# Hybrid attention and recurrence block: where weight loads, a shift row and the first attention stand in the order

## The chip, the core and the metric

The kernel runs on one core of a Trainium2 chip. The time is that of one execution on the device in microseconds (us), as the median of several runs. TensorE (PE) does the matrix products, VectorE (DVE) and ScalarE (ACT) the elementwise work, GpSimd (POOL) some small operations and loads, and SyncE (SP) issues most of the DMA transfers. Each engine, and SP's queue too, takes its instructions in the order in which they were built; an instruction that waits holds up all that stand behind it on the same engine.

## The reference

The block computes one layer on 512 tokens of width 2048, in float32:

```
mod = silu(c) @ w_ada + b_ada                      # six rows of 2048: shift, scale, gate, twice
h   = rms_norm(x, norm1_w) * (1 + scale1) + shift1
aq, ak, av, gq, gf, gi, gg = split(h @ w_in)       # 7 x 1024 columns
attn = rms_norm(dilated_attention(rope(rms(aq)), rope(rms(ak)), av))
hg   = rms_norm(hgrn2(gq, gf, gi)) * silu(gg)      # gated linear recurrence, 8 heads
x    = x + gate1 * (concat(attn, hg) @ w_out)
h2   = rms_norm(x, norm2_w) * (1 + scale2) + shift2
x    = x + gate2 * (square(relu(h2 @ w_ff1)) @ w_ff2)
```

## The kernel before, in words

**Products.** Every float32 operand is split into a high part (a cast on ACT) and a low part (a subtraction on DVE), and each product is the sum of three matmuls: high by high, high by low, low by high. `load_w` (L186) loads two slices of 128 rows by 512 columns of a weight in one DMA of 512 KB into one of four buffers (`wraw`), and `_split` makes `whi` (L39, ACT) and `wlo` (L40, DVE) from each, in four buffers each. `project` (L368) runs over the 16 slices, the steps k: 12 matmuls a step into four PSUM banks, and ACT copies the banks out at the end. There are thirteen such passes over `w_in` after the first two column groups.

**Modulation rows.** The six rows `mod` are matrix by vector products on DVE. `gemv` (L116) loads 256 KB slices (`araw`) and adds each one, times one value per partition, to two accumulators (`acc`, L127 and L129). `to_cols` (L138) adds the two (L143) and has PE turn the row into columns with four transposes (L149); ACT sums them up (L152). Two of these rows, made by `shift_through` (L748), are not of `mod` but of shift1 times columns of `w_in`: the first groups of columns are multiplied before shift1 is known, and what shift1 adds to them is put in afterwards. One is for the forget gates f (columns from 4096), the next for the queries gq of the recurrence (from 3072), and a third (from 4608) stands first in the list `later`.

**Order.** All of this is written as Python generators. `project` calls `tick()` once a step, which advances the front of `tasks` (the recurrence of four heads, or the attention of four heads) by one piece, and `bg_step()` at a rate of 1.85 or 2 a step, which advances `bgw` (the modulation rows). From the first pass after the column groups on (`hv0`, columns from 5120) PE's order is the order in which the code was traced (`manual_schedule`). On the other engines and on SP a scheduler sets the order when the program is built, from priorities and from its own model of time; `load_w` raises the priority of the weight loads. `issue_after(i)` keeps what is traced in its block behind instruction `i` on the same engine.

**Around the change.** The pass `hv0` runs with the shift rows from 4096 and 3072 in `bgw`. After it the recurrence `hgrn` of the first four heads is put into `tasks`; three passes later the attention of the first four heads, which runs through `hgrn_q(1)` (L558) and the next pass; then the second recurrence. In `attention` (L444), `scores` puts the products on DVE (L474, L476), then the exponentials on ACT (L478), `weights_t` transposes them on PE (L490) four pieces later, and `values` multiplies with v (L501).

Of the kernel before, what the change touches and what calls it, by code (L numbers as in the profile page):

```python
# [18 lines left out]
NK = D // P  # L19
# [25 lines left out]
def hybrid_block(ctx, tc, x, c, positions, norm1_w, w_ada, b_ada, w_in, q_norm_w, k_norm_w,  # L45
                 attn_out_norm_w, hg_lb_logits, hg_norm_w, w_out, norm2_w, w_ff1, w_ff2,
                 lnc, hgmask, inv_freq, out):
    nc = tc.nc
# [5 lines left out]
    win_v = w_in[0].rearrange("(k p) n -> p k n", p=P)  # L54
# [13 lines left out]
    def bank(name, tag="bg"):  # L68
        return ps.tile([P, 512], F32, name=name, tag=tag)
# [43 lines left out]
    pool.dma_start(ifq, inv_freq.broadcast_to([P, 16]))  # L113


    def gemv(view, vec, col0, n=512, early=False):  # L116

        accs = [(work("acc") if early else gv.tile([P, 512], F32, name="acc"))[:, 0:n] for _ in range(2)]
        nk = 512 // n
        for k0 in range(0, NK, nk):  # L120
            raw = spare.pop(0) if early and spare else slot("araw") if early else gv.tile([P, 512], F32, name="araw", bufs=4)
            raw = raw.rearrange("p (k n) -> p k n", n=n)
            nc.sync.dma_start(raw, view[:, k0:k0 + nk, col0:col0 + n])
            for k in range(k0, k0 + nk):
                acc = accs[k % 2]
                if k < 2:
                    dve.tensor_scalar(acc, raw[:, k - k0], vec[:, k:k + 1], None, op0=ALU.mult)  # L127
                else:
                    dve.scalar_tensor_tensor(acc, raw[:, k - k0], vec[:, k:k + 1], acc, op0=ALU.mult, op1=ALU.add)  # L129
            yield  # L130
        gemv.acc = accs
# [51 lines left out]
        nc.sync.dma_start(dst.rearrange("o (r p) -> (o r) p", p=P), row[0:NK, 0:P])  # L183
        yield

    def load_w(view, k0, c0, n=512, eng=None, ahead=True, raws=None):  # L186
        with tc.high_priority() if ahead else ExitStack():
            raw = wr.tile([P, 2, n], F32, name="wraw", tag="raw", bufs=4)
            nc.sync.dma_start(raw, view[:, k0:k0 + 2, c0:c0 + n])
            if raws is not None:  # L190
                raws[:] = [raw[:, 0], raw[:, 1]]
            return [_split(nc, wr, raw[:, j], n, eng if j else None) for j in range(2)]
# [35 lines left out]
    def slot(name, dt=F32):  # L228
        return io.tile([P, 512], dt, name=name, tag="io")

    def work(name, dt=F32):
        return wk.tile([P, 512], dt, name=name, tag="wk")
# [83 lines left out]
    shift_done, behind = set(), []  # L316
# [27 lines left out]
    bgw = []  # L344
# [9 lines left out]
    tasks = []  # L354
# [13 lines left out]
    def project(c0, mm, rate=1.85, after=None):  # L368

        banks = [bank("prj", tag="mm") for _ in range(4)]  # L370
        for k0 in range(0, NK, 2):
            for j, (whi, wlo) in enumerate(load_w(win_v, k0, c0, 512, None)):
                k = k0 + j
                mm(banks, hhi[k], hlo[k], whi, wlo, k == 0, k == NK - 1)
                tick()
                owed[0] += rate
                while owed[0] >= 1.0:
                    bg_step()
                    owed[0] -= 1.0
                if after:  # L380
                    after(k)
        return banks

    mix = [None] * NK
# [56 lines left out]
        bgw.insert(0, qk_norm(ts, i, rs))  # L441
        return ts if i else (ts, rs)

    def attention(qr, ks, vs):  # L444
        qs, rsq = qr

        place = {3: (0, 0), 2: (1, 0), 0: (1, 384), 1: (2, 0)}

        def heads_t(h):
            tT = []  # L450
            for i, src in enumerate((qs, ks)):
                pt = bank("ptq")
                for ti in range(NT):
                    pe.transpose(pt[:, ti * P:(ti + 1) * P], src[ti][:, h * DH:(h + 1) * DH], ident)
                t = work("qT")
                act.activation(t, pt, AF.Copy, scale=wcol[:, i:i + 1])
                tT.append(t)
            return tT

        def scores(h, qT, kT):  # L460
            lsum = sm.tile([P, NT], F32, name="lsum")
            m = sm.tile([P, NT], F32, name="m")
            ps_s = [bank("pscore") for _ in range(3)]
            s_sb = [work("s_sb") for _ in range(3)]
            for ti in (3, 2, 0, 1):
                n = (ti + 1) * P
                b, o = place[ti]
                pe.matmul(ps_s[b][:, o:o + n], lhsT=qT[:, ti * P:(ti + 1) * P], rhs=kT[:, 0:n], start=True, stop=True)
            for ti in (3, 2, 0, 1):
                n = (ti + 1) * P  # L470
                b, o = place[ti]
                s = s_sb[b][:, o:o + n]
                with tc.high_priority(offset=400):
                    dve.scalar_tensor_tensor(s, ps_s[b][:, o:o + n], rsq[:, ti, h:h + 1], lnc_sb[:, 512 - n:512],  # L474
                                             op0=ALU.mult, op1=ALU.add)
                    dve.tensor_reduce(m[:, ti:ti + 1], s, axis=AX.X, op=ALU.max)  # L476
                    dve.tensor_scalar(m[:, ti:ti + 1], m[:, ti:ti + 1], -1.0, None, op0=ALU.mult)
                    act.activation(s, s, AF.Exp, bias=m[:, ti:ti + 1], accum_out=lsum[:, ti:ti + 1])  # L478
            return s_sb, lsum

        def weights_t(s_sb):
            p_sb = []
            for b, tis in enumerate(((3,), (2, 0), (1,))):
                pT = bank("pT")
                p_sb.append(work("p_sb"))
                for ti in tis:
                    o = place[ti][1]
                    for sj in range(ti + 1):
                        c = slice(o + sj * P, o + (sj + 1) * P)
                        pe.transpose(pT[:, c], s_sb[b][:, c], ident)  # L490
                n = 256 if b == 2 else 512
                act.copy(p_sb[b][:, 0:n], pT[:, 0:n])
            return p_sb

        def values(h, p_sb, lsum):
            hs = slice(h * DH, (h + 1) * DH)
            po = bank("po")
            for ti in range(NT):
                b, o = place[ti]
                for sj in range(ti + 1):  # L500
                    pe.matmul(po[:, ti * P:(ti + 1) * P], lhsT=p_sb[b][:, o + sj * P:o + (sj + 1) * P],  # L501
                              rhs=vs[sj][:, hs], start=sj == 0, stop=sj == ti)
            dve.reciprocal(lsum, lsum)
            for ti in range(NT):
                dve.tensor_scalar(qs[ti][:, hs], po[:, ti * P:(ti + 1) * P], lsum[:, ti:ti + 1], None, op0=ALU.mult)

        tT = heads_t(0)
        yield
        p_sb = None
        for h in range(4):  # L510
            if h:
                values(h - 1, p_sb, lsum)
            s_sb, lsum = scores(h, *tT)
            for _ in range(4):
                yield
            p_sb = weights_t(s_sb)
            yield
            if h < 3:
                tT = heads_t(h + 1)
                yield  # L520
        values(3, p_sb, lsum)
        yield
# [225 lines left out]
    def shift_through(col0):  # L748

        yield from gemv(win_v, s1c, col0, early=col0 < 4096 + 512)  # L750
        col = sm.tile([P, 8], F32, name="scol", bufs=2)
        yield from to_cols(gemv.acc, col[:, 0:4])
        for h in range(4):
            if col0 == 3072:
                dve.tensor_scalar(col[:, 4 + h:5 + h], col[:, h:h + 1], QS, None, op0=ALU.mult)
                sg = wk.tile([P, 512], F32, name="sg", tag="ev", bufs=2)
                act.activation(sg, hq0[h], AF.Sigmoid, scale=1.0 / QS, bias=col[:, h:h + 1])
                dve.scalar_tensor_tensor(hq0[h], hq0[h], col[:, 4 + h:5 + h], sg, op0=ALU.add, op1=ALU.mult)
            else:
                f, hd = ((f0, h), (f1, 4 + h))[(col0 - 4096) // 512]  # L760
                forget(hd, f[h], f[h], col[:, h:h + 1])
        yield

    bgw += [shift_through(4096), shift_through(3072)]
    bt, bc = first_groups(4096, 3072, scale_block, shift_start)
    f0 = keep(bt, "f")
    hq0 = keep(bc, "gq", QS)
# [74 lines left out]
    q0 = qk(0, "aq", 0)  # L842
    k0_ = qk(1024, "ak", 1)
    v0 = evac(project(2048, tok_mm), "av")
    tasks.append(attention(q0, k0_, v0))
    hq1 = hgrn_q(1)
    hv1 = evac(project(5120 + 512, tok_mm), "gi")
    tasks.append(hgrn(f1, hq1, hv1, hrs[1]))
# [397 lines left out]
    def after(cs):  # L1246

        return {1: cs[5], 5: cs[6], 6: cs[1], 7: cs[7]}
# [78 lines left out]
    for item, following in zip(items, items[1:] + [None]):  # L1327
        stage_, blk, j, i = item
# [13 lines left out]
        if stage_ == 1:  # L1342
            banks, ahead = product(i, hparts, 0, ws, "bg" if first and j < 2 else "mm", False, call)
# [10 lines left out]
        else:  # L1354
            q, c = blk
            banks, ahead = product(i, fparts, c, ws, "mm", i == 2 and c == NC - 1, call)
# [68 lines left out]
```

## Time and profile before

| what | us |
|---|---|
| median of 3 runs | 2282.14 |
| lowest, highest run | 2280.93, 2285.49 |
| the profiled execution: its time | 2284.35 |
| the profiled execution: its span, first to last instruction | 2282.1 |
| PE busy in the span | 2224.0 |
| DVE busy | 1809.7 |
| ACT busy | 1097.6 |
| POOL busy | 443.4 |

The profiled execution shows a mean granted TensorE clock of 0.996. "Busy" leaves out waits; in the timeline an entry in brackets at the end of a row gives the idle time before it and the instruction that ended it. Times in timelines are from the start of the span. Where several equal instructions follow each other, one row stands for them, with their count.

### The profile page before, as it was taken

What the parts mean: (1) busy time and instruction counts of PE and PEld (TensorE: products, weight loads), DVE (VectorE), ACT (ScalarE), POOL (GpSimd) and SP (SyncE); (2) the same over time, 40 slices, a digit from 0 to 9 for tenths busy, and PEclk for the clock granted to TensorE, in tenths of its full rate; (3) what the DMA queues carried; (4) which work ended last, traced back from release to release, by engine and by line L of the source; (5) the groups of instructions that cost most, each with busy time, mean ns of one, the idle gap of its engine ahead of it and who ended that gap; (6) DMA issues with size and microseconds to landing.
All of it is one profiled execution on the core that took longest, in us unless ns stands there. A gap on an engine that the chain in (4) does not pass through costs nothing.

```text
span 2282.1 us, 33105 instructions
## 1 busy us (share of the span) xinstructions
PE 2224.0 (97%) x11769; PEld 1824.9 (80%) x11769; DVE 1809.7 (79%) x2765; ACT 1097.6 (48%) x1950; POOL 443.4 (19%) x664
## 2 busy tenths in 40 slices
PE   4899999999999999999999999999999999999999
PEld 3787877878778888888888888888888888888887
DVE  6999778668786575678658988988897679967878
ACT  5555344443444554547544555555564333443332
POOL 1000022000220000002232323323232222222221
PEclk9999999999999999999999999999999999999999
DMA  9799465546555256747979789889889987998884
GB/s 319 256 329 326 118 192 167 180 153 213 180 163 179 71 189 219 265 131 247 341 258 369 269 330 363 296 297 381 310 293 378 365 304 261 349 355 306 303 297 164
DMA packets 262582, 598.31 MB, mean 262 GB/s; under 512 B 23220, under 2 KB 43968, under 8 KB 262416
## 3 DMA queue, kind: packets, MB, share of 16 engines
q1 hardware_dynamic: 186800, 332.54, 43.3%
q0 software_dynamic: 70720, 254.21, 30.2%
q10 hardware_dynamic: 4896, 9.44, 1.2%
q8 instruction: 93, 1.52, 0.3%
q14 instruction: 73, 0.60, 0.1%
HBM read 518.49 MB, written 77.61 MB: 261 GB/s over the span
## 4 chain that ended last, share of the span: by engine, by line
PE 69%; issue 11%; DMA 11%; DVE 5%; POOL 3%; ACT 1%; SPq 0%; POOLq 0%; DVEq 0%; ACTq 0%
PE prj L198 9%; PE f L1183 9%; PE f L1182 9%; PE f L1181 9%; PE prj L200 9%; PE prj L199 9%; DMA f_lod<-fs 3%; PE f L208 2%; PE f L207 2%; PE f L206 2%; DMA araw<-in_w_ada_dram 2%; DMA araw<-in_w_in_dram 1%; DMA Fl<-f_lod 1%; DMA f_hid<-part 1%; PE prj L207 1%
## 5 line engine op out<-in xcount | busy, mean ns | idle before, releaser
L1165 ACT CAST vhi<-raw 128x1024 fp32r<-128x1024 f32 x392 | 413.4, 1055 | 533.9 <-PE f L1183 420.2
L1166 DVE TENSOR_TENSOR vlo<-raw,vhi 128x1024 fp32r<-128x1024 f32 x392 | 475.9, 1219 | 151.3 <-ACT vhi L1165 150.6
L1182 PE MATMUL f<-vlo,Fh 128*128 128x512 f32 x1376 | 537.0, 390 | 3.4 <-DVE vlo L1166 3.3
L1183 PE MATMUL f<-vhi,Fl 128*128 128x512 f32 x1376 | 535.7, 389 | 0.7 <-DMA Fl<-f_lod 0.7
L1181 PE MATMUL f<-vhi,Fh 128*128 128x512 f32 x1376 | 536.0, 390 | 0.0
L39 ACT CAST whi<-wraw 128x512 fp32r<-128x512 f32 (+1 forms) x368 | 220.0, 601 | 447.5 <-PE prj L200 309.2
L198 PE MATMUL prj<-whi,hi 128*128 128x512 f32 x896 | 365.1, 407 | 3.8 <-ACT gq L564 2.4
L200 PE MATMUL prj<-whi,lo 128*128 128x512 f32 x896 | 351.8, 393 | 0.0
L199 PE MATMUL prj<-wlo,hi 128*128 128x512 f32 x896 | 350.8, 392 | 0.0
L40 DVE TENSOR_TENSOR wlo<-wraw,whi 128x512 fp32r<-128x512 f32 (+1 forms) x368 | 242.4, 663 | 125.8 <-ACT whi L39 120.6
L129 DVE SCALAR_TENSOR_TENSOR acc<-araw,sc,acc 128x512 f32<-128x512 f32 (+1 forms) x392 | 253.2, 671 | 91.1 <-DMA araw<-in_w_ada_dram 90.0
L1182 PEld LDWEIGHTS f<-vlo,Fh 128*128 128x128 f32 x1376 | 258.3, 188 | 61.6 <-DVE vlo L1166 8.7
L1183 PEld LDWEIGHTS f<-vhi,Fl 128*128 128x128 f32 x1376 | 258.4, 188 | 55.0 <-DMA Fl<-f_lod 1.6
L1181 PEld LDWEIGHTS f<-vhi,Fh 128*128 128x128 f32 x1376 | 258.4, 188 | 53.4
L1149 DVE TENSOR_TENSOR raw<-raw,raw 128x1024 f32<-128x1024 f32 x224 | 268.0, 1217 | 3.3 <-DMA raw<-in_w_ff_dram 2.9
L198 PEld LDWEIGHTS prj<-whi,hi 128*128 128x128 f32 x896 | 169.3, 189 | 39.9 <-ACT gq L564 3.6
L200 PEld LDWEIGHTS prj<-whi,lo 128*128 128x128 f32 x896 | 168.9, 188 | 37.0 <-DVE lo L240 0.3
L199 PEld LDWEIGHTS prj<-wlo,hi 128*128 128x128 f32 x896 | 169.5, 189 | 32.4 <-DVE wlo L40 0.4
L1127 POOL DMA_DIRECT2D Fh<-f_hid x112 | 79.0, 705 | 425.8 <-PE f L1183 413.4
L208 PE MATMUL f<-hi,wlo 128*128 128x512 f32 x256 | 99.9, 390 | 1.9 <-DVE wlo L40 1.9
L206 PE MATMUL f<-hi,whi 128*128 128x512 f32 x256 | 100.3, 392 | 0.0
L207 PE MATMUL f<-lo,whi 128*128 128x512 f32 x256 | 99.6, 389 | 0.0
(311 smaller groups left out, 2913.1 us busy)
## 6 DMA issues: line engine op xcount, KB each, us to landing
raw<-in_w_ff_dram SPq DMA_DIRECT2D x224, 512.0 KB, 9.8
araw<-in_w_ada_dram SPq DMA_DIRECT2D x384, 256.0 KB, 4.3
Fh<-f_hid POOLq DMA_DIRECT2D x112, 512.0 KB, 6.7
Fl<-f_lod POOLq DMA_DIRECT2D x112, 512.0 KB, 7.9
wraw<-in_w_in_dram SPq DMA_DIRECT2D x104, 512.0 KB, 3.9
Fh<-h_hid POOLq DMA_DIRECT2D x60, 512.0 KB, 6.3
Fl<-h_lod POOLq DMA_DIRECT2D x60, 512.0 KB, 7.2
f_hid<-part POOLq DMA_DIRECT2D x48, 512.0 KB, 8.0
```

The costliest lines, as they stand in the source:

```text
L39: nc.scalar.copy(hi, src)
L40: (eng or nc.vector).tensor_tensor(lo, src, hi.bitcast(F32), op=ALU.subtract)
L129: dve.scalar_tensor_tensor(acc, raw[:, k - k0], vec[:, k:k + 1], acc, op0=ALU.mult, op1=ALU.add)
L198: pe.matmul(banks[ti], lhsT=hi[:, ts], rhs=whi, start=first, stop=False)
L199: pe.matmul(banks[ti], lhsT=hi[:, ts], rhs=wlo, start=False, stop=False)
L200: pe.matmul(banks[ti], lhsT=lo[:, ts], rhs=whi, start=False, stop=last)
L1149: dve.tensor_tensor(dst, a, b, op=ALU.subtract)
L1165: cast_done.append(act.copy(hi, src))
L1166: split_done.append(dve.tensor_tensor(lo, src, hi.bitcast(F32), op=ALU.subtract))
L1181: pe.matmul(banks[t], lhsT=fh[u][a][:, ts], rhs=whi[:, a], start=first, stop=False)
L1182: pe.matmul(banks[t], lhsT=fh[u][a][:, ts], rhs=wlo[:, a], start=False, stop=False)
L1183: pe.matmul(banks[t], lhsT=fl[u][a][:, ts], rhs=whi[:, a], start=False, stop=end)
```

## The change

Three edits. (1) `project` remembers, after each pair of steps, the last modulation slice that has been asked for, and from the fourth pair on a weight pair's load is kept behind the slice noted three pairs earlier on SP's queue. (2) The two shift rows in `bgw` become one generator, `staggered`: 17 pieces of the first, six of the second, then the rest of the first, and the rest of the second. Piece 18 of the first, which holds its transposes, comes six pieces later; the number of pieces is the same. (3) The first attention yields three times before it begins.

```diff
+    asked, marks = [None], []
+
     def gemv(view, vec, col0, n=512, early=False):
...
-            nc.sync.dma_start(raw, view[:, k0:k0 + nk, col0:col0 + n])
+            asked[0] = nc.sync.dma_start(raw, view[:, k0:k0 + nk, col0:col0 + n])
...
-    def load_w(view, k0, c0, n=512, eng=None, ahead=True, raws=None):
+    def load_w(view, k0, c0, n=512, eng=None, ahead=True, raws=None, behind=False):
         with tc.high_priority() if ahead else ExitStack():
             raw = wr.tile([P, 2, n], F32, name="wraw", tag="raw", bufs=4)
-            nc.sync.dma_start(raw, view[:, k0:k0 + 2, c0:c0 + n])
+            with tc.issue_after(marks[-3].ins) if behind else ExitStack():
+                nc.sync.dma_start(raw, view[:, k0:k0 + 2, c0:c0 + n])
...
         for k0 in range(0, NK, 2):
-            for j, (whi, wlo) in enumerate(load_w(win_v, k0, c0, 512, None)):
+            for j, (whi, wlo) in enumerate(load_w(win_v, k0, c0, 512, None, behind=len(marks) > 2)):
                 k = k0 + j
                 mm(banks, hhi[k], hlo[k], whi, wlo, k == 0, k == NK - 1)
                 tick()
...
+            marks.append(asked[0])
         return banks
...
-    def attention(qr, ks, vs):
+    def attention(qr, ks, vs, lead=0):
...
+        for _ in range(lead):
+            yield
         tT = heads_t(0)
         yield
...
-    bgw += [shift_through(4096), shift_through(3072)]
+    def staggered(a, b, n_a, n_b):
+        for g, n in ((a, n_a), (b, n_b)):
+            for _ in range(n):
+                next(g)
+                yield
+        yield from a
+        yield from b
+
+    bgw.append(staggered(shift_through(4096), shift_through(3072), NK + 1, 6))
...
-    tasks.append(attention(q0, k0_, v0))
+    tasks.append(attention(q0, k0_, v0, 3))
```

What it does to the order, at three places. In all of them the changed kernel's line numbers are a little higher, and the numbers behind names tell tiles apart.

SP's queue, in the pass `hv0`: `wraw_2107` to `wraw_2444` are its eight weight pairs, `araw` are slices for the shift rows. First before, then the change.

```order
L189 DMA wraw_2199<-in_w_in_dram 128x2x512
L189 DMA wraw_2245<-in_w_in_dram 128x2x512
L123 DMA araw_2129<-in_w_in_dram 128x512
L123 DMA araw_2132<-in_w_in_dram 128x512
L123 DMA araw_2147<-in_w_in_dram 128x512
L123 DMA araw_2150<-in_w_in_dram 128x512
L123 DMA araw_2175<-in_w_in_dram 128x512
L189 DMA wraw_2306<-in_w_in_dram 128x2x512
L123 DMA araw_2178<-in_w_in_dram 128x512
L123 DMA araw_2193<-in_w_in_dram 128x512
L123 DMA araw_2196<-in_w_in_dram 128x512
L189 DMA wraw_2352<-in_w_in_dram 128x2x512
```

```order
L192 DMA wraw_2199<-in_w_in_dram 128x2x512
L125 DMA araw_2129<-in_w_in_dram 128x512
L125 DMA araw_2132<-in_w_in_dram 128x512
L125 DMA araw_2147<-in_w_in_dram 128x512
L125 DMA araw_2150<-in_w_in_dram 128x512
L192 DMA wraw_2245<-in_w_in_dram 128x2x512
L125 DMA araw_2175<-in_w_in_dram 128x512
L125 DMA araw_2178<-in_w_in_dram 128x512
L125 DMA araw_2193<-in_w_in_dram 128x512
L125 DMA araw_2196<-in_w_in_dram 128x512
L192 DMA wraw_2292<-in_w_in_dram 128x2x512
```

The fourth pair now stands behind four slices that stood behind it; the fifth (2306 before, 2292 now) has eight slices ahead of it after the third pair, where it had five. Of the 104 full pairs of `w_in`, 18 now have one to four more slices ahead of them on the queue than before, 13 have one or two fewer, and 73 as many.

DVE, in the same pass: `acc_2061` and `acc_2062` belong to the first shift row, 2298 and 2299 (now 2269 and 2270) to the second, 2557 to the third; `lo12` to `lo15` are the low parts of the last four slices of h. Before, then the change:

```order
L129 SCALAR_TENSOR_TENSOR acc_2062<-araw_2242,s1c_112,acc_2062 128x512
L342 TENSOR_TENSOR lo13_1128<-xnT_439,hi13_1127 128x512
L127 TENSOR_SCALAR acc_2299<-araw_2303,s1c_112 128x512
L40 TENSOR_TENSOR wlo_2309<-wraw_2306,whi_2308 128x512
L143 TENSOR_TENSOR acc_2557<-acc_2557,acc_2558 128x512
L342 TENSOR_TENSOR lo14_1189<-xnT_446,hi14_1188 128x512
L342 TENSOR_TENSOR lo15_1194<-xnT_453,hi15_1193 128x512
L129 SCALAR_TENSOR_TENSOR acc_2298<-araw_2328,s1c_112,acc_2298 128x512
L40 TENSOR_TENSOR wlo_2313<-wraw_2306,whi_2312 128x512
L143 TENSOR_TENSOR acc_2061<-acc_2061,acc_2062 128x512
```

```order
L131 SCALAR_TENSOR_TENSOR acc_2062<-araw_2242,s1c_112,acc_2062 128x512
L131 SCALAR_TENSOR_TENSOR acc_2557<-araw_2901,s1c_112,acc_2557 128x512
L129 TENSOR_SCALAR acc_2269<-araw_2271,s1c_112 128x512
L131 SCALAR_TENSOR_TENSOR acc_2558<-araw_2904,s1c_112,acc_2558 128x512
L129 TENSOR_SCALAR acc_2270<-araw_2286,s1c_112 128x512
L345 TENSOR_TENSOR lo12_1123<-xnT_432,hi12_1122 128x512
L40 TENSOR_TENSOR wlo_2295<-wraw_2292,whi_2294 128x512
L145 TENSOR_TENSOR acc_2061<-acc_2061,acc_2062 128x512
```

The final sum of the first row stands six instructions earlier in DVE's order than before. On PE the four transposes that wait for it (L149) stand 36 matmuls later: after ten of the pass's steps, where it was after seven. Those of the second row stay at the pass's end.

ACT, at the end of `hgrn_q(1)`: `gq` are the copies out of that pass's four banks, `s_sb` the exponentials of the attention. Before, then the change:

```order
L39 CAST whi_5218<-wraw_5216 128x512
L478 ACTIVATE s_sb_5048,lsum_5043<-s_sb_5048,m_5044 128x512
L564 COPY gq_5123<-prj_4559 128x512
L478 ACTIVATE s_sb_5049,lsum_5043<-s_sb_5049,m_5044 128x384
L478 ACTIVATE s_sb_5049,lsum_5043<-s_sb_5049,m_5044 128x128
L564 COPY gq_5125<-prj_4560 128x512
L478 ACTIVATE s_sb_5050,lsum_5043<-s_sb_5050,m_5044 128x256
L564 COPY gq_5127<-prj_4561 128x512
L568 ACTIVATE sg_5131<-gq_5123 128x512
```

```order
L39 CAST whi_5199<-wraw_5197 128x512
L496 COPY p_sb_5023<-pT_5022 128x512
L496 COPY p_sb_5030<-pT_5029 128x512
L496 COPY p_sb_5037<-pT_5036 128x256
L570 COPY gq_5079<-prj_4559 128x512
L574 ACTIVATE sg_5087<-gq_5079 128x512
L570 COPY gq_5081<-prj_4560 128x512
L570 COPY gq_5083<-prj_4561 128x512
```

Head 2's exponentials stood ahead of the copies and among them; now they stand behind all four. Head 1's transposed weights (`p_sb`) are what comes ahead.

## The prediction

> **What bounds the kernel now.** I read the page first, then PE's waits, then the stretches around the waits that the change can reach.
>
> ```profile
> PE 2224.0 (97%) x11769; PEld 1824.9 (80%) x11769; DVE 1809.7 (79%) x2765; ACT 1097.6 (48%) x1950; POOL 443.4 (19%) x664
> ```
>
> PE sets the time: it is busy for 97% of the span. What a reordering can win is PE's idle time and the time that it runs at a lower clock. PE's waits from 190 us to 850 us, where all three edits act, are these two and a third of 1.3 us, which is shown below:
>
> ```profile
> PE pc L149 <- DVE acc L143: 4.8, 1, 4.8
> PE prj L198 <- ACT gq L564: 2.4, 2, 2.0
> ```
>
> The first is the transposes of the first shift row, which wait for its sum on DVE. The second is the pass after `hgrn_q(1)`, which waits for banks that ACT has not copied out. The third lies at 811 us, where PE's and ACT's order does not change, and stays. The stretches show what the two cost (columns: busy us of PE, PEld, DVE, ACT, POOL, then the granted clock, DMA share, GB/s):
>
> ```profile
> 186.50:233.50 47.00, 42.14 (x177) 33.86 (x177) 45.97 (x80) 23.48 (x50) 0.53 (x1) 0.93 0.84 295
> 191.00:210.50 19.50, 19.50 (x88) 15.90 (x87) 18.86 (x32) 11.20 (x25) 0.53 (x1) 1.00 1.04 381
> 210.50:220.30 9.80, 4.95 (x15) 3.91 (x15) 9.41 (x17) 4.17 (x11) 0.00 (x0) 0.66 1.05 387
> 470.00:477.00 7.00, 4.56 (x13) 3.12 (x13) 3.61 (x13) 6.20 (x16) 0.00 (x0) 0.76 0.00 0
> ```
>
> Both stretches show a lower clock, 0.66 and 0.76, so each wait costs more than its idle time. And in the first, DVE is busy for 46 of 47 us and the DMA engines are full: there PE waits for DVE's backlog, not for one late instruction.
>
> **The first wait, priced.** PE's timeline, ahead of, in and behind it:
>
> ```profile
> 199.85 0.60 PE L149 MATMUL pc<-ident,acc 128*128 128x128 f32 x4
> 200.21 0.48 PE L198 MATMUL prj<-whi,hi 128*128 128x512 f32 x1
> 200.52 0.39 PE L199 MATMUL prj<-wlo,hi 128*128 128x512 f32 x1
> ...
> 210.29 0.39 PE L200 MATMUL prj<-whi,lo 128*128 128x512 f32 x1
> 215.53 1.12 PE L149 MATMUL pc<-ident,acc 128*128 128x128 f32 x4 [4.85 <-DVE acc L143]
> 216.30 0.78 PE L198 MATMUL prj<-whi,hi 128*128 128x512 f32 x1
> ...
> 220.29 0.47 PE L198 MATMUL prj<-whi,hi 128*128 128x512 f32 x1
> ```
>
> At full clock one matmul starts 0.227 us after the last (the matmul at 210.29 is the 43rd behind that at 200.52, and 9.77 / 43 = 0.227). Undisturbed, the transposes take 0.36 us (199.85 to 200.21) and the first matmul behind them 0.31. So without the wait the transposes would start at 210.52, the first matmul at 210.88, the second at 211.19 and the tenth, which started at 220.29, at 211.19 + 8 x 0.227 = 213.01. The wait costs **7.3 us**: 4.85 idle, the rest at the lower clock.
>
> In the changed order these transposes stand 36 matmuls, 8.2 us, later: PE reaches them at 210.5 + 8.2 = 218.7. Their sum is made no later than before, at 215.5, since it stands six instructions earlier on DVE. That is a cover of over 3 us, so this wait goes.
>
> **What is late next.** PE now reaches the second row's transposes, at the pass's end, 7.3 us earlier, and DVE's backlog is the same. PE's and DVE's rows:
>
> ```profile
> 242.87 0.60 PE L149 MATMUL pc<-ident,acc 128*128 128x128 f32 x4
> 203.22 0.69 DVE L40 TENSOR_TENSOR wlo<-wraw,whi 128x512 fp32r<-128x512 f32 x1 [0.64 <-ACT whi L39]
> 203.83 4.72 DVE L129 SCALAR_TENSOR_TENSOR acc<-araw,s1c,acc 128x512 f32<-128x512 f32 x7
> 208.47 0.48 DVE L127 TENSOR_SCALAR acc<-araw,s1c 128x512 f32<-128x512 f32 x1
> 208.86 0.68 DVE L342 TENSOR_TENSOR lo<-xnT,hi 128x512 fp32r<-128x512 f32 x1
> 209.47 0.74 DVE L129 SCALAR_TENSOR_TENSOR acc<-araw,s1c,acc 128x512 f32<-128x512 f32 x1
> 219.52 0.55 DVE L556 TENSOR_SCALAR f<-f,omlb,lb 128x512 f32<-128x512 f32 x1 [0.39 <-ACT f L555]
> 232.79 0.68 DVE L143 TENSOR_TENSOR acc<-acc 128x512 f32<-128x512 f32 x1
> ```
>
> PE arrives at 242.87 - 7.28 = 235.6. DVE, from the low part that ended at 203.8 up to and with the second row's sum, has in the changed order 25 accumulations of 0.663 (seven fill 203.83 to 208.47), 3 first products of 0.39 (208.47 to 208.86), 18 subtractions or additions of 0.61 (208.86 to 209.47) and eight short ones of 0.2 to 0.5, such as the L556 row, 3.0 together: 16.6 + 1.2 + 11.0 + 3.0 = 31.8 us. It starts at 203.8, or up to 0.6 later, as one cast more stands ahead of the shift columns on ACT. The sum is ready at 235.6 to 236.2: PE waits 0 to 0.6 us there. The list counts four low parts that before stood behind the sum and ran at ACT's pace; now they stand ahead of it, and the last of them needs a weight cast that PE releases 2.7 us before it arrives, enough for a cast, a subtraction and the sum (0.6 + 0.6 + 0.6). DVE's two waits in the old stretch, 0.64 and 0.39, could come on top, so the bounds are 0 and 1.6; I take **0.5 us**, by the count. A gap that short does not lower the clock: after 1.33 us at 811 us the next matmul follows after 0.34, where at the lower clock it takes 0.60 (473.60 to 474.20, below):
>
> ```profile
> 811.42 0.50 PE L198 MATMUL prj<-whi,hi 128*128 128x512 f32 x1 [1.33 <-ACT gg L705]
> 811.76 0.39 PE L199 MATMUL prj<-wlo,hi 128*128 128x512 f32 x1
> ```
>
> **The second wait, priced.**
>
> ```profile
> 462.38 2.32 PE L468 MATMUL pscore<-qT 128*128 128x512 f32 x8
> 469.80 0.39 PE L208 MATMUL prj<-hi,wlo 128*128 128x512 f32 x1
> 472.14 0.50 PE L198 MATMUL prj<-whi,hi 128*128 128x512 f32 x1 [1.95 <-ACT gq L564]
> 473.60 0.79 PE L198 MATMUL prj<-whi,hi 128*128 128x512 f32 x1 [0.49 <-ACT gq L564]
> 474.20 0.63 PE L199 MATMUL prj<-wlo,hi 128*128 128x512 f32 x1
> ...
> 476.63 0.40 PE L199 MATMUL prj<-wlo,hi 128*128 128x512 f32 x1
> 466.55 0.75 DVE L129 SCALAR_TENSOR_TENSOR acc<-araw,sc,acc 128x512 f32<-128x512 f32 x1 [1.39 <-DMA araw<-in_w_ada_dram]
> 467.21 1.92 DVE L474 SCALAR_TENSOR_TENSOR s_sb<-pscore,rs,lnc_sb 128x512 f32<-128x512 f32 x4
> 470.80 0.72 ACT L478 ACTIVATE s_sb<-s_sb,m 128x512 f32<-128x512 f32 x1 [2.90 <-DVE m L477]
> 471.53 0.56 ACT L564 COPY gq<-prj 128x512 f32<-128x512 f32 x1
> ```
>
> PE had head 2's scores at about 464.5. On DVE they stand behind accumulations that wait for their slices, and begin at 467.21. The exponential at 470.80 waits for them, and the bank copy at 471.53 stands behind it on ACT. Without that, the matmul at 472.14 would start at 470.03 and the eleventh, at 476.63, at 470.03 + 10 x 0.227 = 472.30: **4.3 us**.
>
> With three steps of lead head 2's scores come on PE after the pass has ended, and ACT has the four copies ahead of its exponentials. What now stands ahead of them, head 1's three `p_sb` copies, answers transposes a full step (2.7 us) before the pass's end. I count this wait as gone, with 0 to 0.5 us left.
>
> [...]
>
> **The edit on the loads.** In the pass `hv0` the fifth pair went out at 192.96 and its step begins at 213.2 with the wait gone (210.52 + 12 x 0.227): 20.2 us. Landing takes 8.2 at worst, cast and subtraction some 1.3 (the L40 row has 0.69, the cast is taken alike), so a load could come 10.7 us later and PE would not see it. The rule itself holds a pair behind slices asked for three pairs, 16 us of PE, ahead.
>
> ```profile
> 192.96 0.38 SPq L189 DMA_DIRECT2D wraw<-in_w_in_dram  x1
> DMA to landing us min/median/max: 3.6/3.9/8.2
> SPq L123 <- DVE acc L129: 126.6, 198, 2.3
> SPq L123 <- DVE acc L127: 44.3, 24, 6.6
> ```
>
> One to four more slices ahead of 18 pairs cost by these rows at most 2.3 us each as a rule, four of them 9.2: under 10.7. I count 0. A gain there is bounded too: slices come earlier, but in the first stretch DVE has no room to use that, and in the second the wait is already counted as gone.
>
> **The attention's end** moves by 36 matmuls. The rows of the chain
>
> ```profile
> 507.08 2.23 PE po L501 x20
> 534.30 0.69 PE pA L577 x50
> ```
>
> are its last products and the first of the next recurrence: 27 us apart, and 8.2 are taken. Nothing there is pushed; from there on PE's order is as before.
>
> **Sum.** 7.3 + 4.3 - 0.5 = 11.1 us. Against the profiled execution's 2284.35 that is 2273.3; this execution lies 2.2 above the median of 2282.14, so the forecast is **2271.0**. Behind 850 us PE's order is the same and PE sets the pace, so what is won there is kept to the end. With the bounds (1.6 at the second row, 0.5 at the copies) 2270.5 to 2272.7.
>
> **Rivals.** *The wait moves to the second row.* The counted sum leaves PE no slack there. If DVE also waits for slices, as it does elsewhere in this region, or the DMA engines, full from 191 to 220, land them later, PE waits several us more and the clock falls. At the size of the first wait's idle, 4.85 for 0.5, plus its 2.45 of slow matmuls: 11.1 - 4.35 - 2.45 = 4.3 won, 2278. For it: DVE's 46 of 47 us. Against: DVE is late there by its own work, and SP no longer holds four slices behind a pair that waits for its buffer.
>
> *The slow matmuls behind the second wait stay.* If they have another cause than the gap, only the idle 1.95 + 0.49 is won: 11.1 - 1.9 = 9.2, so 2273. [...]
>
> *Weights come late: slower.* The place is SP: a pair held behind a slice that waits for its buffer by 6.6 us and three more of 2.3 has lost 13.5 of its 10.7 us, and PE waits 2.8, plus some 1.9 at the lower clock: 4.7 a time. From three times on (14.1) it outweighs the gain; with four, 18.8 - 11.1, the time is 2290. For it: 18 pairs moved back. Against: the 6.6 occurs seldom, and most of the 18 move by two or three slices.
>
> **Chances.** The forecast 0.62; the second row 0.14; slow matmuls 0.06; late weights 0.08; smaller leftovers, between 2273 and 2278, 0.10. A measurement here tells changes over 0.2%, 4.6 us, from none: faster is below 2277.6. That takes the forecast, the slow matmuls and the leftovers, 0.78; the second row is mostly "same", 0.13; slower 0.09. The range goes from 2267, as the runs before scatter by some 2 us to either side, up to 2279 with the second row in it.
>
> **What will show it.** Right: no wait of L149 for L143 near 219 us and one below 1.6 us near 236; no wait of L198 for L564; clock 1.00 in both stretches; the wait at 811 us now near 800. Wrong: a wait of PE or of a cast for `wraw`, a wait of several us near 236, or a clock below 1 there.

## The result, and the profile after

| | before | changed |
|---|---|---|
| median, us, measured side by side | 2282.23 | 2273.56 |
| lowest, highest of 5 | 2280.93, 2287.92 | 2272.39, 2274.99 |
| profiled execution: time | 2284.35 | 2273.89 |
| profiled execution: span | 2282.1 | 2272.1 |
| mean granted clock | 0.996 | 0.998 |

The changed kernel takes 0.9956 of the time before, 95% interval 0.9944 to 0.9967: 8.7 us less by the medians, 10.0 by the spans. The forecast was 2271.0.

In the changed kernel, PE's waits between 190 and 850 us (in all, times, longest) are these three:

```profile
PE pc L151 <- DVE acc L145: 0.6, 1, 0.6
PE pr L182 <- DVE aq L509: 1.6, 1, 1.6
PE prj L201 <- ACT gg L711: 1.3, 1, 1.3
```

The first is the second shift row's transposes, where 0.5 was forecast. The third is the old wait of 811 us. The second is new, and the prediction does not have it. The wait of the pass for the copies `gq` (now L570) is gone. The stretches of the changed kernel (busy us of PE, PEld, DVE, ACT, POOL, then the granted clock, DMA share, GB/s):

```profile
186.50:233.50 47.00, 46.99 (x211) 38.27 (x210) 45.88 (x79) 25.36 (x55) 0.53 (x1) 1.00 0.86 297
210.50:220.30 9.80, 9.80 (x46) 8.05 (x45) 9.80 (x17) 3.75 (x8) 0.00 (x0) 1.00 1.00 355
470.00:477.00 7.00, 7.00 (x32) 5.79 (x32) 2.25 (x4) 2.91 (x9) 0.00 (x0) 1.00 0.25 75
```

PE is busy without a break where it was busy for 42.14 of 47 us (the 0.56 us of the second row lie just behind this stretch, at 234.5), and both stretches that had clocks of 0.66 and 0.76 have 1.00.

**A measure finer than the whole time.** Spans of executions scatter by some us from other parts of the program. So I compare PE's way from the first matmul of the pass `hv0` to the matmul behind the wait for `gg` at 800 us, between which all three edits act. The two rows of before, then the two of the changed kernel:

```profile
188.76 0.50 PE L198 MATMUL prj<-whi,hi 128*128 128x512 f32 x1
...
811.42 0.50 PE L198 MATMUL prj<-whi,hi 128*128 128x512 f32 x1 [1.33 <-ACT gg L705]
```

```profile
187.67 0.50 PE L201 MATMUL prj<-whi,hi 128*128 128x512 f32 x1
...
800.84 0.50 PE L201 MATMUL prj<-whi,hi 128*128 128x512 f32 x1 [1.33 <-ACT gg L711]
```

622.66 us before, 613.17 changed: **9.49 us** won there, where the prediction's sum has 11.1. What lies behind the second matmul takes 1470.7 us before and 1471.3 changed, and 1469.3 to 1474.9 in the runs below, so the gain is kept to the end within that scatter.

**The new wait.** PE in the changed kernel; heads are counted from 0. L505 is `values` of head 0 with its result `po`, L472 the scores of head 1, L182 the transpose that turns the finished gate row, one of the modulation rows, into 16 rows:

```profile
437.40 2.39 PE L505 MATMUL po<-av,p_sb 128*128 128x128 f32 x20
439.63 2.32 PE L472 MATMUL pscore<-qT 128*128 128x512 f32 x8
443.50 0.28 PE L182 MATMUL pr<-ident,gcol 128*16 128x128 f32 x1 [1.55 <-DVE aq L509]
...
444.08 0.39 PE L211 MATMUL prj<-hi,wlo 128*128 128x512 f32 x1
444.31 0.39 PE L209 MATMUL prj<-hi,whi 128*128 128x512 f32 x1
```

The small transpose needs a PSUM bank, a tile for PE's results, from the pool of four that `bank()` gives out beside the passes' four. `po` holds one of them, the three score tiles the others, and the fifth tile takes `po`'s bank, which comes free when DVE has made `aq` from it. DVE:

```profile
438.53 0.75 DVE L131 SCALAR_TENSOR_TENSOR acc<-araw,sc,acc 128x512 f32<-128x512 f32 x1 [0.89 <-DMA araw<-in_w_ada_dram]
439.75 0.75 DVE L131 SCALAR_TENSOR_TENSOR acc<-araw,sc,acc 128x512 f32<-128x512 f32 x1 [0.47 <-DMA araw<-in_w_ada_dram]
441.66 0.75 DVE L131 SCALAR_TENSOR_TENSOR acc<-araw,sc,acc 128x512 f32<-128x512 f32 x1 [0.55 <-DMA araw<-in_w_ada_dram]
442.33 1.12 DVE L509 TENSOR_SCALAR aq<-po,lsum 128x128 f32<-128x128 f32 x4
```

`aq` ends at 443.45 and PE goes on at 443.50. `aq` stands behind accumulations that wait for their slices, 1.9 us in these three rows; that is how slices hold up PE here. The transpose itself did not move in PE's order: the third edit put the values of head 0 and the scores of head 1 right ahead of it.

With that the terms add up: 7.3 - 0.6 + 4.3 - 1.55 = 9.45, against 9.49 on the way.

### The profile page after: what moved, and what is told of

Its sections match the earlier page's. It is cut to its first block, busy times and chain, and to the rows that moved or that the text cites. A ratio compares the mean times of both kernels' runs of the same rounds, so it can differ in the third digit from the quotient of the medians.

```text
span 2272.1 us, 33110 instructions
## 1 busy us (share of the span) xinstructions
PE 2219.7 (98%) x11769; PEld 1821.1 (80%) x11769; DVE 1809.6 (80%) x2765; ACT 1097.3 (48%) x1950; POOL 441.8 (19%) x664
## 4 chain that ended last, share of the span: by engine, by line
PE 70%; DMA 10%; DVE 8%; issue 8%; POOL 2%; ACT 1%; SPq 0%; POOLq 0%; DVEq 0%; ACTq 0%
PE f L1197 9%; PE f L1196 9%; PE f L1195 9%; PE prj L201 8%; PE prj L203 8%; PE prj L202 8%; DMA araw<-in_w_ada_dram 3%; PE f L211 2%; PE f L209 2%; PE f L210 2%; DVE vlo L1180 2%; DMA f_lod<-fs 2%; DVE raw L1163 2%; PE prj L209 1%; PE prj L210 1%
```

## The experiments

Theory after the result: the two old waits cost 7.3 and 4.3 us with their slow matmuls and went, by the second and the third edit; the first edit is worth nothing; the third made a new wait for a bank. The prediction's rivals stood against it, and some of their own for each run. In the table, "way" is the stretch defined above, "ratio" is against the kernel before on the same chip, and the diffs below are against the changed kernel.

| kernel | median us | ratio, 95% interval | way us | won on the way |
|---|---|---|---|---|
| before | 2282.23 | | 622.66 | |
| changed | 2273.56 | 0.9956, 0.9944 to 0.9967 | 613.17 | 9.49 |
| e1 second edit alone | 2279.34 | 0.9974, 0.9964 to 0.9983 | 615.35 | 7.31 |
| e2 third edit alone | 2282.90 | 0.9993, 0.9984 to 1.0002 | 620.81 | 1.85 |
| e3 first edit alone | 2276.06 | 0.9964, 0.9951 to 0.9976 | 616.56 | 6.10 |
| e4 without the first | 2273.64 | 0.9955, 0.9943 to 0.9968 | 614.66 | 8.00 |
| e5 changed, again | 2274.06 | 0.9960, 0.9948 to 0.9972 | 613.94 | 8.72 |
| e6 lead of four | 2272.90 | 0.9951, 0.9939 to 0.9964 | 612.38 | 10.28 |
| e7 lead of two | 2271.77 | 0.9946, 0.9934 to 0.9958 | 611.17 | 11.49 |
| e8 second edit alone, two pieces | 2279.28 | 0.9983, 0.9973 to 0.9994 | 619.32 | 3.34 |
| e9 lead of two, without the first | 2272.70 | 0.9942, 0.9927 to 0.9957 | 611.20 | 11.46 |
| e10 lead of two, again | 2272.37 | 0.9941, 0.9927 to 0.9955 | 611.67 | 10.99 |

Before stood at 2284.60 beside e1 to e4, 2284.44 beside e5 to e8 and 2285.29 beside e9 and e10.

**e1: the second edit alone.**

```diff
-            for j, (whi, wlo) in enumerate(load_w(win_v, k0, c0, 512, None, behind=len(marks) > 2)):
+            for j, (whi, wlo) in enumerate(load_w(win_v, k0, c0, 512, None, behind=False)):
...
-    tasks.append(attention(q0, k0_, v0, 3))
+    tasks.append(attention(q0, k0_, v0))
```

> Only the second edit: the first shift row's transposes six pieces later; loads and attention as before. Theory (the prediction's first term, with the 0.6 that the changed kernel showed at the second row): the wait of L149 near 210 us goes with its slow matmuls, 7.3 us, and 0.6 comes back at the second row's transposes: 6.7 us won, 2275.5. The wait of the pass behind hgrn_q(1) stays with 1.95 + 0.49 us of idle, some 7 us earlier. Rival one: the slow matmuls behind the gap have another cause than the gap, and only the idle 4.85 is won: 4.3 us, 2278. Rival two: without the first edit the pairs of hv0 keep DVE's and SP's old order, and the second row's sum comes later than 0.6 us: each us more there is a us less won, and above some 2 us the clock falls near 236 us.

Waits of e1 from 186 to 520 us:

```profile
PE pc L151 <- DVE acc L145: 0.3, 1, 0.3
PE prj L201 <- ACT gq L570: 2.3, 2, 1.8
```

The theory's 7.0 (7.3 - 0.3) stands against 7.31. Rival one would have given 4.3 to 4.5 and falls, and so does rival two. The first row's sum ended at 214.6 here and PE reached its transposes at 217.81: the cover of 3 us that the prediction gave.

**e2: the third edit alone.**

```diff
-            for j, (whi, wlo) in enumerate(load_w(win_v, k0, c0, 512, None, behind=len(marks) > 2)):
+            for j, (whi, wlo) in enumerate(load_w(win_v, k0, c0, 512, None, behind=False)):
...
-    bgw.append(staggered(shift_through(4096), shift_through(3072), NK + 1, 6))
+    bgw.extend([shift_through(4096), shift_through(3072)])
```

> Only the third edit: the first attention three steps later; loads and shift rows as before. Theory (the prediction's third term, with the wait that the changed kernel showed): the wait of the pass behind hgrn_q(1) goes with its slow matmuls, 4.3 us, and the gate row's transpose, which now stands right behind head 1's scores, waits 1.6 us for a bank: 2.7 us won, 2279.5; the wait of 4.85 us at 210 us stays. Rival one, the prediction as it stood: 4.3 us, 2278. Rival two (the matmuls behind the old wait were slow for another reason than the gap): 2.4 - 1.6 = 0.8 us, 2281.4, and slow matmuls remain near 472 us.

The wait for `gq` is gone and the one at the gate row is there, but it cost more than its idle time. PE of e2:

```profile
449.02 0.28 PE L182 MATMUL pr<-ident,gcol 128*16 128x128 f32 x1 [2.02 <-DVE aq L509]
...
449.99 0.63 PE L209 MATMUL prj<-hi,whi 128*128 128x512 f32 x1
450.41 0.63 PE L210 MATMUL prj<-lo,whi 128*128 128x512 f32 x1
...
453.24 0.40 PE L211 MATMUL prj<-hi,wlo 128*128 128x512 f32 x1
```

From 449.99 on matmuls start 0.42 us apart. The twelfth behind the transpose starts at 453.24, 4.2 us after the first; in the changed kernel that took 2.6. So the new wait costs 2.02 + 1.6 = 3.6 of the 4.3 won, and by this sum the third edit alone is worth 0.7. Of the 1.85 on the way, 0.76 belongs to the old wait at 210 us, whose idle time is still 4.85 but behind which the slow stretch was shorter: it ended 3.6 us after the wait's end, in before 4.8. (From the start of `hv0` to the second row's transposes e2 takes 53.35 us, before 54.11.) That leaves 1.1 for the third edit, 0.4 more than the sum. By medians the run can't be told from before. The theory named both waits rightly and gave the net gain too large, since it counted the new wait at its idle time.

**e3: the first edit alone.**

```diff
-    bgw.append(staggered(shift_through(4096), shift_through(3072), NK + 1, 6))
+    bgw.extend([shift_through(4096), shift_through(3072)])
...
-    tasks.append(attention(q0, k0_, v0, 3))
+    tasks.append(attention(q0, k0_, v0))
```

> Only the first edit: pairs kept behind slices; shift rows and attention as before. Theory (the prediction counted 0 for this edit): both old waits stay as they were, 4.85 us at 210 us and 1.95 + 0.49 us at 472 us, and the time is 2282, within 1 us. Rival one: on DVE the first row's sum stands six rows earlier by this edit alone, as in the changed kernel, where it was ready at 211.1 us and before at 215.5 us; then most of the wait at 210 us goes already here: up to 6 us won, 2276. Rival two: pairs come late, PE waits for casts of late pairs: over 2284.

The theory, nothing, is wrong and rival one is right: 6.10 us on the way, with an interval of the ratio that leaves no doubt. PE's transposes and DVE's sums in e3:

```profile
210.77 0.66 PE L151 MATMUL pc<-ident,acc 128*128 128x128 f32 x4 [1.62 <-DVE acc L145]
...
210.02 0.69 DVE L145 TENSOR_TENSOR acc<-acc 128x512 f32<-128x512 f32 x1
213.09 0.69 DVE L145 TENSOR_TENSOR acc<-acc 128x512 f32<-128x512 f32 x1
```

DVE's sums in before:

```profile
211.73 0.68 DVE L143 TENSOR_TENSOR acc<-acc 128x512 f32<-128x512 f32 x1
214.80 0.68 DVE L143 TENSOR_TENSOR acc<-acc 128x512 f32<-128x512 f32 x1
```

Two sums stand near each other, those of the first and of the third row. In before the third row's, for which nobody waits at that time, comes first and the first row's 3.07 us later; with the first edit they have changed places in DVE's order. The wait falls from 4.85 to 1.62, and no slow matmuls follow it: 7.3 - 1.6 = 5.7. The other 0.4 is at the copies `gq`, where the idle time was 2.7 without slow matmuls.

**e4: the second and third edits without the first.**

```diff
-            for j, (whi, wlo) in enumerate(load_w(win_v, k0, c0, 512, None, behind=len(marks) > 2)):
+            for j, (whi, wlo) in enumerate(load_w(win_v, k0, c0, 512, None, behind=False)):
```

> The second and third edits without the first. Theory: the first edit is worth nothing once the two waits are gone, so the time is that of the changed kernel, 2273.6, within 1 us, with the waits 0.6 at the second row and 1.6 at the gate row. Rival: the first edit lets slices come earlier, and without it DVE's sums are late: a wait of 1 to 3 us near 236 us, or more than 1.6 us at the gate row's transpose, 2275 to 2277.

2273.64 by median, as expected. On the way it is 1.5 us longer than the changed kernel, and that lies at the gate row: a wait of 2.00 with slow matmuls behind it (twelve matmuls in 4.1 us, 1.5 more than in the changed kernel). 7.3 - 0.3 + 4.3 - 2.0 - 1.5 = 7.8, against 8.00. Whether the first edit shortens that wait isn't told by one execution; e5 and e9 answer that.

**e5: the changed kernel again.**

> The changed kernel itself, timed beside the next three on one chip. Expected as it was: 2273.6 within 1.5 us, and the waits 0.6 at the second row and 1.6 to 2.0 at the gate row's transpose. By the theory that a gap over some 1.75 us lowers the clock (1.69 did not, 1.80 did), 512-column matmuls stay 0.23 us apart behind a gate-row gap below 1.7 and start 0.42 us apart behind one above 1.8.

```profile
446.48 0.28 PE L182 MATMUL pr<-ident,gcol 128*16 128x128 f32 x1 [2.70 <-DVE aq L509]
...
446.82 0.40 PE L210 MATMUL prj<-lo,whi 128*128 128x512 f32 x1
447.06 0.40 PE L211 MATMUL prj<-hi,wlo 128*128 128x512 f32 x1
```

In this execution of the same kernel the gate row's wait is 2.70 us, where it was 1.55 and where e4 and e2 had 2.0: its length varies from run to run, with the slices on which DVE waits: the last of its waits ahead of `aq` is 2.18 us here and was 0.55. So e4's 2.00 is no evidence for the first edit. And the expectation on the clock is wrong: behind 2.70 us of idle matmuls start 0.24 us apart, at full clock, while 1.80, 2.00 and 2.02 were followed by slow ones. The last section comes back to this.

**e6 and e7: a lead of four, a lead of two.** Both keep all three edits.

```diff
-    tasks.append(attention(q0, k0_, v0, 3))
+    tasks.append(attention(q0, k0_, v0, 4))
```

> The changed kernel with four steps of lead in place of three: the gate row's transpose then stands 12 matmuls ahead of head 1's values and scores. Theory (the transpose waited for a bank that those had taken): its wait of 1.55 us goes and nothing takes its place, since head 1's exponentials end some 2 us ahead of the pass: 1.5 us faster than the changed kernel, 2272. Rival one: the transpose waited for the gate row itself, which is late by DVE's late slices, and waits as long or longer where it stands earlier: no gain. Rival two: the copies gq now stand right behind head 1's exponentials, and the old wait of the pass's end comes back with 2 to 4 us: 2274 to 2277.

```diff
-    tasks.append(attention(q0, k0_, v0, 3))
+    tasks.append(attention(q0, k0_, v0, 2))
```

> The changed kernel with two steps of lead: the gate row's transpose stands 12 matmuls behind head 1's scores. Theory: 2.7 us of matmuls cover the 1.55 us for which it waited for the bank, so this wait goes; head 2's scores come in the last step of hgrn_q(1) and their exponentials behind the copies gq, so the old wait stays away: 2272. Rival one: the transpose waits for the gate row itself, not for the bank, and that comes at the same time as before: its place is later here too, so only a wait shorter by 2.7 us is seen, the same; it is told apart by the run with four steps. Rival two: copies gq wait behind head 1's transposed weights and the pass's end waits 1 to 2 us: 2273 to 2275.

In both the gate row's wait is gone. With a lead of four the transpose stands 12 matmuls ahead of the values (head 0's, where the expectation has head 1's) and scores and doesn't wait: the row itself was there in time, so rival one falls, and the bank was what it waited for. What is left there is a trace of rival two:

```profile
457.03 0.50 PE L201 MATMUL prj<-whi,hi 128*128 128x512 f32 x1 [0.17 <-ACT gq L570]
459.04 0.50 PE L201 MATMUL prj<-whi,hi 128*128 128x512 f32 x1 [0.36 <-ACT gq L570]
```

With a lead of two nothing is left. PE's scores and transpose, and DVE's `aq`, in e7:

```profile
436.63 2.32 PE L472 MATMUL pscore<-qT 128*128 128x512 f32 x8
...
441.56 0.27 PE L182 MATMUL pr<-ident,gcol 128*16 128x128 f32 x1
...
437.90 1.12 DVE L509 TENSOR_SCALAR aq<-po,lsum 128x128 f32<-128x128 f32 x4
```

The bank is free at 439.0, and PE comes at 441.6. The way is 2.0 us shorter than in the changed kernel: 11.49, where 7.3 - 0.6 + 4.3 gives 11.0. The median of e7 is 2.3 us below that of e5 on the same chip, but the two intervals of the ratio overlap; the difference is shown by the way, not by the whole time.

**e8: the second edit alone, with two pieces in place of six.** This puts the first row's transposes 12 matmuls later.

```diff
-            for j, (whi, wlo) in enumerate(load_w(win_v, k0, c0, 512, None, behind=len(marks) > 2)):
+            for j, (whi, wlo) in enumerate(load_w(win_v, k0, c0, 512, None, behind=False)):
...
-    bgw.append(staggered(shift_through(4096), shift_through(3072), NK + 1, 6))
+    bgw.append(staggered(shift_through(4096), shift_through(3072), NK + 1, 2))
...
-    tasks.append(attention(q0, k0_, v0, 3))
+    tasks.append(attention(q0, k0_, v0))
```

> The second edit alone at a smaller size: the first row's transposes two pieces later, 12 matmuls, where the change has six pieces and 36 matmuls. Theory (the wait is the sum's time less PE's arrival): 4.85 - 12 x 0.227 = 2.1 us of wait remain near 212 us, and as that is over 1.8 the matmuls behind it are slow for some 3 us, which costs 1.5 to 2.5 more: of the 7.3 us some 3 are won, 2279 by the profiled execution of before. [...] Rival two: DVE's backlog moves along with the transposes: the wait stays near 4.8.

```profile
214.41 0.66 PE L151 MATMUL pc<-ident,acc 128*128 128x128 f32 x4 [2.13 <-DVE acc L145]
...
215.37 0.39 PE L203 MATMUL prj<-whi,lo 128*128 128x512 f32 x1
215.60 0.55 PE L201 MATMUL prj<-whi,hi 128*128 128x512 f32 x1
215.95 0.63 PE L202 MATMUL prj<-wlo,hi 128*128 128x512 f32 x1
216.38 0.63 PE L203 MATMUL prj<-whi,lo 128*128 128x512 f32 x1
...
219.25 0.39 PE L201 MATMUL prj<-whi,hi 128*128 128x512 f32 x1
219.48 0.40 PE L202 MATMUL prj<-wlo,hi 128*128 128x512 f32 x1
```

The wait is 2.13, to the hundredth what 4.85 - 12 x 0.227 gives: DVE's backlog stays where it is and PE's arrival alone decides. Rival two falls. The nine matmuls from 215.60 to 219.25 take 3.65 us where they take 2.04 at full clock, 1.6 more, so 7.3 - 2.1 - 1.6 = 3.6; the way shows 3.34.

**e9 and e10: a lead of two without the first edit, and with it again.**

```diff
-            for j, (whi, wlo) in enumerate(load_w(win_v, k0, c0, 512, None, behind=len(marks) > 2)):
+            for j, (whi, wlo) in enumerate(load_w(win_v, k0, c0, 512, None, behind=False)):
...
-    tasks.append(attention(q0, k0_, v0, 3))
+    tasks.append(attention(q0, k0_, v0, 2))
```

> The second edit and the third with two steps of lead, without the first. Theory: the first edit moves the first shift row's sum 3 us earlier, which is worth up to 6 us where PE arrives at it early, and nothing where the transposes stand 36 matmuls later; the time is that of the run with all edits and two steps of lead, 2271.8 within 1 us, and PE's way from the first matmul of hv0 to the matmul behind the wait at 800 us takes 611.2 us within 0.4, as there. Rival: the first edit also brings later slices earlier, and without it a wait of 0.5 to 2 us comes up behind 250 us: 612 to 613.5 us on that way.

> The version with all three edits and two steps of lead once more, beside the run without the first edit. Expected: 2271.8 within 1 us, PE's way from the first matmul of hv0 to the matmul behind the wait at 800 us 611.2 us within 0.3, no wait at the gate row's transpose and none for the copies gq. If the gate row's bank were only just free in time there, a wait of up to 1 us shows, as the same wait was 1.55 us in one execution of the changed kernel and 2.70 us in another.

The ways are 611.20 without the first edit, 611.17 and 611.67 with it, and the waits on it are 0.3 or 0.6 at the second row and 1.3 at 800 us, no others. So beside the other two edits the first one is worth nothing, and e7's time repeats. The kernel with the second edit and a lead of two is as good as any measured here.

## Why the prediction was right or wrong

**Direction and range** held: 2273.56 lies between 2267 and 2279, and the gain is over 0.2%. The forecast itself was 2.6 us too low, from two steps.

**The first wait, 7.3: right.** The transposes came at 217.55, the sum was ready at 211.1, the clock is 1.00. e1 gives 7.31 on the way and e8, at a third of the move, the wait that the same rows give. The prediction put the sum at 215.5 at the latest, which is its time without the first edit.

**What is late next, 0.5: right.** 0.56 in the changed kernel, 0.3 to 0.6 in all others with six pieces.

**The second wait, 4.3: right, and replaced.** It is gone with 0 left, as forecast. But the paragraph on the attention's end ("Nothing there is pushed") looked only at the far end of what moved. The step that failed is the listing of what the third edit moves: it followed head 1's `p_sb` and head 2's scores, and not the values of head 0 and the scores of head 1, which now stand right ahead of the gate row's transpose and hold the four banks from which it needs one. That adds 1.55 us here, 2.70 in another execution, and 3.5 to 3.6 where the clock fell too. The rows for it were there before: PE's order showed the new neighbours, and DVE's waits of up to 1.39 us for slices ahead of `s_sb` showed how late DVE empties such banks. e6 and e7, which take only these neighbours apart, win 0.8 and 2.0 us more than the changed kernel, and e7's 11.49 (10.99 in e10) is what the sum of 11.1 would have been right for.

**The offset to the median: wrong size.** The prediction took 2.2 us off since the profiled execution of before lay that far above its median. For the changed kernel it lies 0.3 above. Against its own execution the forecast was 2273.3, measured 2273.89: there the new wait was nearly made up by what other parts of that execution gave, such as the 1.1 us by which `hv0` began earlier.

**The edit on the loads, 0: right in the sum, wrong as a statement on the edit.** Beside the other two it changes nothing (e9, e10). Alone it wins 6.10, since it makes the first row's sum 3.07 us earlier. The prediction had that move, "six instructions earlier on DVE", and used it only as more cover for the second edit. Its price of 2.3 us a slice goes by SP's waits for `acc`; it leaves out those put down to earlier slices still on their way, up to 5.6 us in before, and no pair came late all the same. The two edits are two cures of one wait: alone 6.1 and 7.3, together not 13.4.

**The rivals.** The wait did not move to the second row with several us. Weights did not come late: from 186 to 860 us no wait of PE for `whi` or `wlo` shows. The slow matmuls behind the second wait did not stay: the stretch from 470 to 477 has a clock of 1.00, and e1, which keeps the wait, has slow matmuls again behind 1.80 and 0.49 us: its way is 2.2 us longer than the changed kernel's, with 0.5 us more of idle time. Gaps from 1.80 to 2.63 us were followed by slow matmuls, and one of 2.70 was not (last section).

## What to carry to other kernels

When a block of work is moved along an in-order engine, look also at the instructions that did not move: their new neighbours may hold the buffers that they need, and a four-bank pool with a five-bank demand turns a tiny transpose into a stall of 1.55 to 2.7 us. Two edits that cure the same wait don't add, so each is worth a run alone and a run left out; here one of the three could be dropped and another made smaller. A few us in 2280 are read better from one engine's way between two fixed instructions around the change than from medians that scatter by as much.

## What the runs showed of the hardware that was not expected

Whether a gap lowers PE's clock isn't decided by its length alone. Idle times and what followed them, on the way:

| gap, us | where | 512-column matmuls behind it |
|---|---|---|
| 1.55 | changed, gate row | 0.23 us apart |
| 1.62 | e3, first row | 0.23 apart |
| 1.69, then 0.48 and 0.56 | e3, copies | 0.23 apart |
| 1.80, then 0.49 | e1, copies | slow, some 1.7 us lost |
| 1.95, then 0.49 | before, copies | slow, 0.42 apart |
| 2.00 | e4, gate row | slow, twelve in 4.1 us |
| 2.02 | e2, gate row | slow, 0.42 apart |
| 2.13 | e8, first row | slow, 0.43 apart |
| 2.63 | e8, copies | slow until 471.75 |
| 2.70 | e5, gate row | 0.24 apart |
| 4.85 | before, first row | slow, 0.43 apart |
| 4.85 | e2, first row | slow |

The 1.7 us of e1 are an estimate: the 2.2 by which its way is longer than the changed kernel's, less the 0.5 of idle time. The 2.70 of e5 left the clock as it was: the granted clock is 1.00 from 441.19 to 451.43, ahead of the gap, in it and behind it. And the same 4.85 us was followed by slow stretches of different length: the slow matmuls ended 4.8 us after the gap in before and 3.6 in e2. In before the granted clock is 0.50 from 215.53 to 220.29 and 1.00 from 220.60 to 223.00.

The slow stretches end, and in e8 (at 215.60) and e2 (by 449.99) also begin, in the midst of equal matmuls, where nothing in the program changes. In e8 one ends at 219.25, the next, behind another gap, at 471.75:

```profile
471.37 0.54 PE L202 MATMUL prj<-wlo,hi 128*128 128x512 f32 x1
471.75 0.40 PE L203 MATMUL prj<-whi,lo 128*128 128x512 f32 x1
```

In before they end at 101.00, 220.60 and 476.63; up to the first row of each pair matmuls start 0.43 us apart, and behind the second 0.23 to 0.24:

```profile
100.58 0.59 PE L207 MATMUL prj<-lo,whi 128*128 128x512 f32 x1
101.00 0.40 PE L208 MATMUL prj<-hi,wlo 128*128 128x512 f32 x1
...
220.29 0.47 PE L198 MATMUL prj<-whi,hi 128*128 128x512 f32 x1
220.60 0.40 PE L199 MATMUL prj<-wlo,hi 128*128 128x512 f32 x1
...
476.33 0.46 PE L198 MATMUL prj<-whi,hi 128*128 128x512 f32 x1
476.63 0.40 PE L199 MATMUL prj<-wlo,hi 128*128 128x512 f32 x1
```

What decides whether a gap lowers the clock, and for how long, was not shown: these are executions as they fell. What it means for estimates is measured: the gate row's gap of 2.0 to 2.7 us cost its own length, or some 1.5 us more.
